# One decoder layer on one core: which engine makes the normalised x, and where in VectorE's queue it stands

## The chip, the cores and the metric

The kernel runs on one core of a Trainium2 chip. The metric is the device time of one execution in microseconds (us), as the median of several runs. The engines are TensorE (PE in the profile, its weight loads PEld), VectorE (DVE), ScalarE (ACT), GpSimd (POOL) and SyncE (SP, which issues the transfers). Each works through its own queue in order and waits on semaphores for the others.

## The reference

One layer of a decoder with 256 tokens and a model width of 1,024. The residual stream is normalised (RMSNorm) and multiplied by one wide matrix; the pieces of the product feed a mixture of dilated window attentions (A), a block attention (B), attention to 256 memory tokens (M), gates and merge logits. Cut to the part that the change touches:

```python
h = rmsnorm(x, norm_w[l])              # x * rsqrt(mean(x^2) + eps) * w
proj = h @ w_in[l]
pieces = jnp.split(proj, IN_SPLIT_POINTS, axis=-1)
...
kv = rmsnorm(mem, mem_norm_w[l]) @ w_mem_kv[l]
...
merged = g_a * p_a + g_b * p_b + g_m * p_m
x = x + merged @ w_out[l]
return rmsnorm(x, final_norm_w)
```

## The kernel before

Everything is fp32, but TensorE multiplies rounded values. So every operand `a` is split into a rounded upper part and the remainder, the lower part, and a product takes three matmuls: upper by upper, upper by lower, lower by upper. For a weight chunk, `split_cols` makes `wh` (upper, ScalarE, L93) and `wl` (lower, VectorE, L94).

The weights come in chunks of 1 MB, in the order of `PLAN` (L60). `load` (L79) issues a chunk's transfer three chunks ahead into one of three `wraw` buffers; `split` makes its upper and lower part in halves (from chunk 4 on) two chunks ahead. `wh` has three buffers and `wl` two, so `wl` of chunk i is written over that of chunk i-2. Chunks 0 to 5 are the query, key and value of branch B, two chunks each (`Bq`, `Bk`, `Bv`); 6 and 7 are gates of B, 8 to 10 gates of A and M, 11 and 12 the memory's key and value.

The normalisation needs a sum over the whole row, which is known late. Chunks 0 to 5 therefore multiply x times the norm's weights alone, `xh` and `xl` (L154, L155), and their results are scaled by the row's factor `rb["x"]` as they leave PSUM (`evac_b`, L546, L549, L541). From chunk 6 on the operand is the normalised x itself, `hh` and `hl`. `make_h` (L191) computes it into `h32`, one slice `k` of 128 features by 256 tokens at a time: x times the norm's weight of the feature `nw`, times the token's factor `rb`. Tokens are reordered on the way into four classes of position (`CLASSES`), so that both operands are read at every fourth element. Slices 0 and 1 are made on VectorE, in two halves each (L200); slices 2 to 7 on GpSimd in two steps, the weight in place (L196) and then the factor (L197). `split_h` (L203) splits four slices at a time: `hh` on ScalarE (L204), `hl` on VectorE (L205).

The loop over chunks (L554 on) calls, in iteration i: the transfer of chunk i+3; the first half of chunk i+2's split; the matmuls of chunk i, with the second half of the split between its two halves; and then, for the B chunks from 3 on, `evac_b`, at i = 3 `make_h` for all slices, and at i = 4 and 5 `split_h`. The order in which each engine's queue gets its instructions is not simply that of the program: it is settled when the program is built (L763), by a planner that goes by the program's order and by its own estimate of when each instruction can start. `x` transposed lies in `xp`, whose place is later taken by the memory `memT`; `h32` shares its place with the natural layouts of x before it and of the memory (`memn`) behind it. The two transfers of `mem_load` (L209) so wait for the last readers of x and `h32`.

Of the kernel before, what the change touches and what calls it, by code (L numbers as in the profile page):

```python
# [7 lines left out]
F32 = mybir.dt.float32  # L8
# [3 lines left out]
ALU = mybir.AluOpType  # L12
# [5 lines left out]
KD = D // P  # L18
# [9 lines left out]
CLASSES = "p (i r e) -> p e r i"  # L28
# [35 lines left out]
def kernel(ctx: ExitStack, tc: tile.TileContext, wts: bass.AP, xT_d: bass.AP, memT_d: bass.AP,  # L64
                      x_d: bass.AP, mem_d: bass.AP, xr_d: bass.AP, fnw_d: bass.AP, con_d: bass.AP, out: bass.AP):
    nc = tc.nc
# [5 lines left out]
    pa = ctx.enter_context(tc.tile_pool(name="pa", bufs=2, space=PSUM))  # L72

    NCH = len(PLAN)
    raws, whs, wls = {}, {}, {}
    width = [1024 if PLAN[i][0] == "W" and PLAN[i][2] == "m" else 2048 for i in range(NCH)]
    offs = [sum(width[:i]) * P for i in range(NCH + 1)]

# [8 lines left out]
    def split_cols(i, lo, hi):  # L87
        if lo == 0:
            o = place(i)
            whs[i] = wp.tile([P, 2112], F32R, tag="wh", name=f"wh{i}")[:, o:o + 2048]  # L90
            wls[i] = wp.tile([P, 2112], F32R, tag="wl", bufs=2, name=f"wl{i}")[:, o:o + 2048]
        sl = slice(lo, hi)
        nc.scalar.copy(whs[i][:, sl], raws[i][:, sl])  # L93
        nc.vector.tensor_tensor(wls[i][:, sl], raws[i][:, sl], whs[i][:, sl].bitcast(F32), op=ALU.subtract)  # L94

    def split(i, part, parts):
        n = width[i] // parts
        split_cols(i, part * n, (part + 1) * n)

    def place(i):  # L100


        return 32 if PLAN[i][0] in ("Av", "Bv", "Mv", "O") else 0
# [9 lines left out]
    par, xT = xp[:, 0:40], xp[:, 40:].rearrange("p (k t) -> p k t", k=KD)  # L113
    for i in range(2):
        raws[i] = wp.tile([P, 2048], F32, tag="wraw", name=f"wraw{i}")
        src0 = wts[offs[i]:offs[i + 1]].rearrange("(p c) -> p c", p=P)
        for j in range(4):
            k = 4 * i + j
# [21 lines left out]
    nw = par[:, 0:8]  # L140
# [12 lines left out]
    for k in range(KD):  # L153
        nc.scalar.activation(xh[:, k, :], xT[:, k, :], AF.Copy, scale=nw[:, k:k + 1])  # L154
        nc.vector.scalar_tensor_tensor(xl[:, k, :], xT[:, k, :], nw[:, k:k + 1], xh[:, k, :].bitcast(F32),  # L155
                                       op0=ALU.mult, op1=ALU.subtract)
        if k:
            split(k // 4, k % 4, 4)
        else:
            split(0, 0, 8)  # L160
            split(0, 1, 8)
# [29 lines left out]
    def make_h(lo, hi):  # L191
        rbp = rb["x"].rearrange(CLASSES, e=2, r=2)
        for k in range(lo, hi):
            hk = h32[:, k].rearrange("p e (r i) -> p e r i", r=2)
            if k >= 2:
                nc.gpsimd.tensor_scalar(xT[:, k, :], xT[:, k, :], nw[:, k:k + 1], 1.0, op0=ALU.mult, op1=ALU.mult)  # L196
                nc.gpsimd.tensor_tensor(hk, xT[:, k, :].rearrange(CLASSES, e=2, r=2), rbp, op=ALU.mult)  # L197
                continue
            for e in range(2):
                nc.vector.scalar_tensor_tensor(hk[:, e], xT[:, k, :].rearrange(CLASSES, e=2, r=2)[:, e], nw[:, k:k + 1],  # L200
                                               rbp[:, e], op0=ALU.mult, op1=ALU.mult)

    def split_h(lo, hi):  # L203
        nc.scalar.copy(hh[:, lo:hi], h32[:, lo:hi])  # L204
        nc.vector.tensor_tensor(hl[:, lo:hi], h32[:, lo:hi], hh[:, lo:hi].bitcast(F32), op=ALU.subtract)  # L205
# [67 lines left out]
    def split_q(src, scale, name):  # L273

        xs = []
        for s in range(2):
            own, other = halves(s)
            t = rp.tile([P, 512], F32R, tag="r", name=f"{name}x{s}")
            nc.scalar.mul(t[own], src[own], scale)
            nc.vector.scalar_tensor_tensor(t[other], src[own], scale, t[own].bitcast(F32), op0=ALU.mult,  # L280
                                           op1=ALU.subtract)
            xs.append(t)
        return [t.rearrange("p (f t) -> p f t", f=2) for t in xs]
# [269 lines left out]
    for i, (kind, key, src, col) in enumerate(PLAN):  # L553
# [54 lines left out]
        if kind[0] == "B":  # L608
            late.append((i, kind, key) + ((pss[2 * i], pss[2 * i + 1]) if i < 2 else (ps, None)))
            if i >= 3:  # L610
                for z in [z for z in late if i == 5 or z[0] > 1]:
                    evac_b(*z)
                    late.remove(z)
                if i == 3:
                    make_h(0, KD)
                else:
                    split_h(4 * i - 16, 4 * i - 12)
        elif kind in ("Aq", "Ak", "Av", "Mq", "Mk", "Mv"):
            at = (kind,) + (key if kind[0] == "A" else (0,))
            if kind[1] == "q" and at[-1] == 0:  # L620
                qkv[at] = split_q(ps, -SCALE, f"{kind}{i}")
            elif kind[1] == "k" and at[-1] == 0:
                qkv[at] = split_k(ps, f"{kind}{i}")
            elif kind == "Av" and key[1] > 0:

                hf, g = key
                if g == 1:
                    stacked[hf] = tp.tile([P, 2, 2, S], F32, tag="vs", name=f"vs{hf}")
                for r in range(2):
                    nc.scalar.copy(stacked[hf][64 * (g - 1):64 * g, :, r, :],  # L630
                                   ps[64 * r:64 * (r + 1)].rearrange("p (e c) -> p e c", e=2))
            else:
                t = qkv[at] = rtile(f"{kind}{i}")
                nc.scalar.mul(t, ps, -SCALE if kind == "Aq" else 1.0)
        elif kind == "G":
            th = tp.tile([P, 512], F32, tag="th", name="thg")
            nc.scalar.activation(th, ps, AF.Tanh, scale=0.5)
            g = gate[key] = rp.tile([P, 512], F32, tag="g", name=f"g{i}", bufs=5)
            nc.vector.scalar_tensor_tensor(g, th, 1.0, ps, op0=ALU.add, op1=ALU.mult)
        elif kind == "L":  # L640
            br, bk = key
            th = ths[br, bk] = tp.tile([P, 512], F32, tag="th", name="thl")
            off = {"a": 0, "b": 8, "m": 16}[br]
            for n in range(2):
                c = off + 2 * bk + n
                nc.scalar.activation(th[:, S * n:S * (n + 1)], ps[:, S * n:S * (n + 1)], AF.Tanh, bias=hb[:, c:c + 1],
                                     scale=0.5)
        elif kind == "W":
            br, hf = key
            kn = 2 if br == "m" else 4  # L650
            oh = [og[br, k][0] for k in range(kn)]
            ol = [og[br, k][1] for k in range(kn)]
            if "t" not in acc:
                acc["t"] = cp.tile([P, 4, 512], F32, tag="xt", name="acc")
            for j in range(2):
                bk = 2 * hf + j
                ps = pj.tile([P, 512], F32, tag="pj", name=f"pw{i}{j}")
                for n in range(2):
                    mm_feat(ps, S * n, i, kn, 512, 2 * j + n, oh, ol)
                    if j == 1 and n == 0 and i + 2 < NCH:  # L660
                        split(i + 2, 1, 2)
                a = acc["t"][:, bk, :]
                if br == "b":
                    nc.vector.scalar_tensor_tensor(a, ths[br, bk], 1.0, ps, op0=ALU.add, op1=ALU.mult)
                else:
                    tmp = tp.tile([P, 512], F32, tag="mt", name="mt", bufs=1)
                    nc.vector.scalar_tensor_tensor(tmp, ths[br, bk], 1.0, ps, op0=ALU.add, op1=ALU.mult)
                    if br == "m":
                        nc.gpsimd.tensor_tensor(a, a, tmp, op=ALU.add)
                    else:  # L670
                        nc.vector.tensor_tensor(a, a, tmp, op=ALU.add)
                        mh = rp.tile([P, 2, S], F32R, tag="r", name=f"mgh{bk}")
                        ml = rp.tile([P, 2, S], F32R, tag="r", name=f"mgl{bk}")
                        nc.scalar.copy(mh.rearrange("p a b -> p (a b)"), a)
                        nc.vector.tensor_tensor(ml.rearrange("p a b -> p (a b)"), a,
                                                mh.rearrange("p a b -> p (a b)").bitcast(F32), op=ALU.subtract)
                        merged[bk] = (mh, ml)
                if j == 0:
                    pump(i, 0)
        else:  # L680
            if key < 2:
                order = [(key, i, 0), (key, i, 1)]
            elif key == 2:
                order = [(key, i, 0)]
            else:
                order = [(key, i, 0), (key - 1, i - 1, 1), (key, i, 1)]
            with tc.manual_schedule(engines={mybir.EngineType.PE}) if key == 3 else ExitStack():
                for kc, wi, t in order:
                    out_mm(kc, wi, t)
                    if t == 0 and i + 2 < NCH:  # L690
                        split(i + 2, 1, 2)
                    if kc == 3:
                        finish(t)
# [73 lines left out]
```

## Time and profile before

| what | value |
| --- | --- |
| median of 3 runs | 355.07 us (354.67 to 355.75) |
| the profiled execution | 353.61 us |
| its span, first to last instruction | 351.8 us |
| mean granted TensorE clock | 0.991 |
| busy: TensorE, VectorE, ScalarE, GpSimd | 339.3, 237.0, 206.4, 35.1 us |

The profile is one execution. The span leaves out what lies before the first instruction and after the last. The granted clock is TensorE's, as a share of full speed. Matmuls overlap one another, so a matmul's duration is longer than the time from its start to the next one's.

### The profile page before, as it was taken

What the parts mean: (1) busy time and instruction counts of PE and PEld (TensorE: products, weight loads), DVE (VectorE), ACT (ScalarE), POOL (GpSimd) and SP (SyncE); (2) the same over time, 40 slices, a digit from 0 to 9 for tenths busy, and PEclk for the clock granted to TensorE, in tenths of its full rate; (3) what the DMA queues carried; (4) which work ended last, traced back from release to release, by engine and by line L of the source; (5) the groups of instructions that cost most, each with busy time, mean ns of one, the idle gap of its engine ahead of it and who ended that gap; (6) DMA issues with size and microseconds to landing.
All of it is one profiled execution on the core that took longest, in us unless ns stands there. A gap on an engine that the chain in (4) does not pass through costs nothing.

```text
span 351.8 us, 7109 instructions
## 1 busy us (share of the span) xinstructions
PE 339.3 (96%) x2924; PEld 324.5 (92%) x2924; DVE 237.0 (67%) x401; ACT 206.4 (59%) x367; POOL 35.1 (10%) x44
## 2 busy tenths in 40 slices
PE   8995999999999999999999999999999999999992
PEld 4995999999999998999999999999999999999882
DVE  3859979998898963446886352766544747567554
ACT  6665669867768664637766362864643465546222
POOL 1409200000001000000101000010000213000022
PEclk9999899999999999999999999999999999999998
DMA  7995695846334353445343635434334376645003
GB/s 211 312 411 197 259 386 202 322 149 232 129 126 153 135 203 118 168 136 224 122 132 115 228 126 197 164 129 159 133 121 169 132 241 238 234 143 224 0 2 120
DMA packets 12945, 63.33 MB, mean 180 GB/s; under 512 B 1392, under 2 KB 2800, under 8 KB 6640
## 3 DMA queue, kind: packets, MB, share of 16 engines
q1 hardware_dynamic: 12912, 62.88, 50.0%
q8 instruction: 23, 0.38, 0.4%
q14 instruction: 10, 0.08, 0.1%
HBM read 61.82 MB, written 1.05 MB: 179 GB/s over the span
## 4 chain that ended last, share of the span: by engine, by line
PE 88%; DMA 5%; DVE 3%; ACT 1%; SPq 1%; issue 0%; POOL 0%; POOLq 0%; DVEq 0%
PE pj L240 17%; PE pj L241 16%; PE pj L243 16%; PE pj L260 5%; PE pj L261 5%; PE pj L262 5%; PE pt L328 3%; PE pw L240 3%; DMA wraw<-in_wts 3%; PE pw L241 3%; PE pw L243 3%; DMA xn<-in_x 2%; PE y L501 2%; PE y L500 2%; PE y L499 2%; DVE h L200 1%
## 5 line engine op out<-in xcount | busy, mean ns | idle before, releaser
L94 DVE TENSOR_TENSOR wl<-wraw,wh 128x1024 fp32r<-128x1024 f32 (+2 forms) x117 | 131.5, 1159 | 65.1 <-issue 52.0
L93 ACT CAST wh<-wraw 128x1024 fp32r<-128x1024 f32 (+2 forms) x117 | 107.9, 967 | 45.9 <-PE pj L241 27.3
L240 PE MATMUL pj<-hh,wh 128*128 128x256 f32 x480 | 115.2, 281 | 0.0
L241 PE MATMUL pj<-hl,wh 128*128 128x256 f32 x480 | 113.8, 279 | 0.0
L240 PEld LDWEIGHTS pj<-hh,wh 128*128 128x128 f32 x480 | 90.4, 188 | 1.0 <-issue 0.6
L241 PEld LDWEIGHTS pj<-hl,wh 128*128 128x128 f32 x480 | 90.5, 188 | 0.4 <-issue 0.4
L243 PE MATMUL pj<-hh,wl 128*128 128x256 f32 x480 | 65.9, 279 | 0.0
L243 PEld LDWEIGHTS pj<-hh,wl 128*128 128x128 f32 x480 | 60.0, 188 | 0.0
L260 PE MATMUL pj<-wh,hh 128*128 128x256 f32 x96 | 27.0, 281 | 0.0
L262 PE MATMUL pj<-wh,hl 128*128 128x256 f32 x96 | 26.9, 280 | 0.0
L261 PE MATMUL pj<-wl,hh 128*128 128x256 f32 x96 | 26.7, 278 | 0.0
L320 ACT ACTIVATE u<-u,st 128x384 f32<-128x384 f32 (+2 forms) x32 | 16.9, 529 | 13.1 <-DVE st L314 13.1
L329 ACT COPY ptsb<-pt 128x384 f32<-128x384 f32 (+1 forms) x28 | 13.1, 495 | 11.4 <-PE pt L328 11.1
L260 PEld LDWEIGHTS pj<-wh,hh 128*128 128x128 f32 x96 | 18.1, 189 | 0.5 <-issue 0.4
L262 PEld LDWEIGHTS pj<-wh,hl 128*128 128x128 f32 x96 | 18.0, 188 | 0.4 <-issue 0.4
L261 PEld LDWEIGHTS pj<-wl,hh 128*128 128x128 f32 x96 | 18.0, 188 | 0.0
L362 POOL TENSOR_SCALAR nba<-con 128x512 f32<-128x512 f32 x8 | 5.0, 620 | 126.8 <-DVE st L314 125.9
L322 DVE TENSOR_SCALAR u<-u,st 128x256 f32<-128x256 f32 (+2 forms) x40 | 16.4, 416 | 0.9
L501 PE MATMUL y<-wh,mgl 128*128 128x512 f32 (+1 forms) x40 | 14.0, 350 | 0.0
L500 PE MATMUL y<-wl,mgh 128*128 128x512 f32 (+1 forms) x40 | 14.0, 350 | 0.0
L499 PE MATMUL y<-wh,mgh 128*128 128x512 f32 (+1 forms) x40 | 14.0, 349 | 0.0
L261 PE MATMUL pj<-wl,xh 128*128 128x256 f32 x32 | 9.9, 309 | 3.8 <-DVE wl L94 3.8
(196 smaller groups left out, 568.5 us busy)
## 6 DMA issues: line engine op xcount, KB each, us to landing
wraw<-in_wts SPq DMA_DIRECT2D x48, 1024.0 KB, 4.8
wraw<-in_wts SPq DMA_DIRECT2D x15, 256.0 KB, 6.1
xn<-in_x SPq DMA_DIRECT2D x1, 1024.0 KB, 8.4
memT<-in_memT SPq DMA_DIRECT2D x1, 1024.0 KB, 8.0
memn<-in_mem SPq DMA_DIRECT2D x1, 1024.0 KB, 8.6
xres<-in_xr SPq DMA_DIRECT2D x1, 1024.0 KB, 4.9
wraw<-in_wts SPq DMA_DIRECT2D x2, 512.0 KB, 3.2
out<-ysb SPq DMA_DIRECT2D x4, 256.0 KB, 2.1
```

The source lines that it names most:

```text
L93: nc.scalar.copy(whs[i][:, sl], raws[i][:, sl])
L94: nc.vector.tensor_tensor(wls[i][:, sl], raws[i][:, sl], whs[i][:, sl].bitcast(F32), op=ALU.subtract)
L240: nc.tensor.matmul(ps[:, lo:lo + S], wh[:, k, fs], ah[k], start=(k == 0), stop=False)
L241: nc.tensor.matmul(ps[:, lo:lo + S], wh[:, k, fs], al[k], start=False, stop=False)
L243: nc.tensor.matmul(ps[:, lo:lo + S], wl[:, k, fs], ah[k], start=False, stop=(k == kn - 1))
L260: nc.tensor.matmul(ps[:, lo:lo + S], ah[k], wh[:, k, :], start=(k == 0), stop=False)
L261: nc.tensor.matmul(ps[:, lo:lo + S], ah[k], wl[:, k, :], start=False, stop=False)
L262: nc.tensor.matmul(ps[:, lo:lo + S], al[k], wh[:, k, :], start=False, stop=(k == KD - 1))
L320: nc.scalar.activation(u[:, lo:hi], src[:, lo:hi], AF.Exp, bias=st[:, 0:1], scale=-1.0, accum_out=st[:, 1:2])
L499: nc.tensor.matmul(y[t, n][:, 0:w], ht, wh[:, k, cs], start=(kc == 0 and k == 0), stop=False)
L500: nc.tensor.matmul(y[t, n][:, 0:w], ht, wl[:, k, cs], start=False, stop=False)
L501: nc.tensor.matmul(y[t, n][:, 0:w], lt, wh[:, k, cs], start=False, stop=(kc == 3 and k == 1))
```

## The change

GpSimd multiplies all eight slices of x by the norm's weights, in place, in the loop that makes `xh` and `xl`. `make_h` has one VectorE instruction for a slice, whatever its number. It is called for four slices at i = 3 and for the other four at i = 4, and its VectorE instructions are put behind the last lower-part instruction of chunk i+1 in VectorE's queue (`issue_after`: an order within the queue, not a semaphore). At i = 4 `split_h` of the first four slices stands ahead of `make_h` of the last four.

```diff
-    raws, whs, wls = {}, {}, {}
+    raws, whs, wls, lower = {}, {}, {}, {}
...
-        nc.vector.tensor_tensor(wls[i][:, sl], raws[i][:, sl], whs[i][:, sl].bitcast(F32), op=ALU.subtract)
+        lower[i] = nc.vector.tensor_tensor(wls[i][:, sl], raws[i][:, sl], whs[i][:, sl].bitcast(F32), op=ALU.subtract)
...
         nc.vector.scalar_tensor_tensor(xl[:, k, :], xT[:, k, :], nw[:, k:k + 1], xh[:, k, :].bitcast(F32),
                                        op0=ALU.mult, op1=ALU.subtract)
+        nc.gpsimd.tensor_scalar(xT[:, k, :], xT[:, k, :], nw[:, k:k + 1], 1.0, op0=ALU.mult, op1=ALU.mult)
...
             hk = h32[:, k].rearrange("p e (r i) -> p e r i", r=2)
-            if k >= 2:
-                nc.gpsimd.tensor_scalar(xT[:, k, :], xT[:, k, :], nw[:, k:k + 1], 1.0, op0=ALU.mult, op1=ALU.mult)
-                nc.gpsimd.tensor_tensor(hk, xT[:, k, :].rearrange(CLASSES, e=2, r=2), rbp, op=ALU.mult)
-                continue
-            for e in range(2):
-                nc.vector.scalar_tensor_tensor(hk[:, e], xT[:, k, :].rearrange(CLASSES, e=2, r=2)[:, e], nw[:, k:k + 1],
-                                               rbp[:, e], op0=ALU.mult, op1=ALU.mult)
+            nc.vector.tensor_tensor(hk, xT[:, k, :].rearrange(CLASSES, e=2, r=2), rbp, op=ALU.mult)
...
-                if i == 3:
-                    make_h(0, KD)
-                else:
+                if i > 3:
                     split_h(4 * i - 16, 4 * i - 12)
+                if i < 5:
+
+                    with tc.issue_after(lower[i + 1].ins):
+                        make_h(4 * i - 12, 4 * i - 8)
```

## Rows read from the trace of the kernel before

**Rows 1.** The page: busy time of each engine, its share of the span, instructions.

```profile
PE 339.3 (96%) x2924; PEld 324.5 (92%) x2924; DVE 237.0 (67%) x401; ACT 206.4 (59%) x367; POOL 35.1 (10%) x44
```

**Rows 2.** TensorE's waits: engine, line, whom it waited for; total us, times, longest.

```profile
PE pj L261 <- DVE wl L94: 3.8, 1, 3.8
```

**Rows 3.** Stretches of the span: length, busy time of each engine, clock, transfers.

```profile
core 0: us, PE busy (x) PEld busy (x) DVE busy (x) ACT busy (x) POOL busy (x), PEclk, DMA share, GB/s
...
22.90:30.40 7.50, 6.91 (x55) 6.45 (x54) 6.64 (x11) 4.93 (x9) 4.41 (x4) 1.00 1.00 389
30.40:34.20 3.80, 0.05 (x1) 0.05 (x1) 3.80 (x4) 2.11 (x3) 3.80 (x4) 1.00 0.17 69
34.20:38.40 4.20, 4.20 (x22) 4.16 (x23) 4.20 (x4) 3.77 (x4) 3.61 (x3) 0.59 0.21 59
...
47.00:66.00 19.00, 19.00 (x168) 18.95 (x167) 18.47 (x25) 18.50 (x28) 0.71 (x1) 1.00 0.75 271
```

**Rows 4.** Timeline of TensorE: start, duration (us), instruction, [idle before it, its releaser].

```profile
23.95 0.38 PE L240 MATMUL pj<-xh,wh 128*128 128x256 f32 x1 [0.58 <-ACT wh L93]
...
30.11 0.28 PE L260 MATMUL pj<-wh,xh 128*128 128x256 f32 x1
34.15 0.39 PE L261 MATMUL pj<-wl,xh 128*128 128x256 f32 x1 [3.76 <-DVE wl L94]
...
46.21 0.28 PE L262 MATMUL pj<-wh,xl 128*128 128x256 f32 x1
...
47.04 0.28 PE L240 MATMUL pj<-hh,wh 128*128 128x256 f32 x1
...
77.28 0.28 PE L241 MATMUL pj<-ml,wh 128*128 128x256 f32 x1
```

**Rows 5.** Timeline of ScalarE.

```profile
26.59 2.00 ACT L93 CAST wh<-wraw 128x1024 fp32r<-128x1024 f32 x2
...
57.60 1.06 ACT L171 ACTIVATE memn<-memn 128x1024 f32<-128x1024 f32 x1
```

**Rows 6.** Timeline of VectorE, instructions of one kind in a row merged.

```profile
27.33 4.67 DVE L200 SCALAR_TENSOR_TENSOR h<-xp,rb_x 128x128 f32<-128x128 f32 x4
...
37.47 0.68 DVE L549 SCALAR_TENSOR_TENSOR Bk<-pj,rb_x 128x512 f32<-128x512 f32 x1
38.06 2.35 DVE L94 TENSOR_TENSOR wl<-wraw,wh 128x1024 fp32r<-128x1024 f32 x2
40.33 1.21 DVE L205 TENSOR_TENSOR hl<-h,hh 128x1024 fp32r<-128x1024 f32 x1
...
42.66 1.41 DVE L546 SCALAR_TENSOR_TENSOR Bq<-pj,rb_x 128x256 f32<-128x256 f32 x4
...
47.17 2.36 DVE L94 TENSOR_TENSOR wl<-wraw,wh 128x1024 fp32r<-128x1024 f32 x2 [1.97 <-issue]
...
67.56 3.25 DVE L224 SCALAR_TENSOR_TENSOR memT<-memT,small,rb_m 128x256 f32<-128x256 f32 x8
...
74.80 1.30 DVE L228 TENSOR_TENSOR ml<-memT,mh 128x512 fp32r<-128x512 f32 x2
```

**Rows 7.** Single instructions of VectorE and GpSimd in the timeline, 30 to 36 us.

```profile
30.67 1.33 DVE L200 SCALAR_TENSOR_TENSOR h<-xp,rb_x 128x128 f32<-128x128 f32 x1
30.47 1.29 POOL L197 TENSOR_TENSOR h<-xp,rb_x 128x256 f32<-128x256 f32 x1
...
31.92 2.17 DVE L94 TENSOR_TENSOR wl<-wraw,wh 128x1024 fp32r<-128x1024 f32 x1
31.73 1.29 POOL L197 TENSOR_TENSOR h<-xp,rb_x 128x256 f32<-128x256 f32 x1
...
34.02 2.19 DVE L94 TENSOR_TENSOR wl<-wraw,wh 128x1024 fp32r<-128x1024 f32 x1
```

**Rows 8.** Instructions of L196: shortest, median, longest in ns, first and last start.

```profile
L196 POOL TENSOR_SCALAR xp<-xp x6: 477/667/880, 8.3 to 15.2; 128x256 f32<-128x256 f32 x6
```

**Rows 9.** Timeline of the queue that issues transfers.

```profile
41.58 0.38 SPq L211 DMA_DIRECT2D memn<-in_mem  x1
```

**Rows 10.** The page's transfers: size, median us from issue to landing.

```profile
memn<-in_mem SPq DMA_DIRECT2D x1, 1024.0 KB, 8.6
```

## The prediction

> **What bounds the kernel now.** I read the page first, then the waits of TensorE, then the stretches around the one long wait, then the queues one by one.
>
> TensorE is busy for 339.3 us, 96% of the span [rows 1], so time can be won only where TensorE waits or runs slowly. The list of its waits names one long wait in the whole span: 3.8 us, for the lower part `wl` of a weight chunk, on VectorE [rows 2]. The table by stretch shows it at 30.4 to 34.2 us: TensorE does one instruction, VectorE and GpSimd are busy throughout. [...]
>
> TensorE's own timeline says what it waited for. At 30.11 us it starts chunk 4 (`Bv`, first half) with the product of upper parts (L260); the next product (L261) needs `wl` of chunk 4 and comes at 34.15 us. Chunk 6, the first to need `hh` and `hl`, starts at 47.04 us [rows 4].
>
> VectorE's queue says why `wl` was late. ScalarE rounds chunk 4's upper part from 26.59 to 28.6 us [rows 5], so `wl` could start at about 27.6. VectorE's program order, however, has four L200 instructions first: 4.67 us from 27.33 [rows 6], while GpSimd makes the other six slices. `wl` of chunk 4 starts at 31.92, and its two halves take 2.17 and 2.19 us [rows 7], where two halves of a later chunk take 2.35 us together [rows 6].
>
> The single records of the two engines show them taking turns. GpSimd's L197 instructions start at 30.47 and 31.73, VectorE's at 30.67 and 31.92 [rows 7]. Both records of 1.3 us are mostly waiting: between 30.47, when one GpSimd instruction ended, and 30.67, when VectorE's ended, VectorE had 0.20 us; again 0.19 us between 31.73 and 31.92. GpSimd had 30.67 to 31.73, which is 1.06 us. So a strided half slice (128 columns) is worth about 0.2 us on VectorE alone, and a strided slice (256 columns) about 1.06 us on GpSimd.
>
> **The change part by part.**
>
> *GpSimd's multiplication by the norm's weights.* Six such instructions exist already; they run between 8.3 and 15.2 us, 0.48 to 0.88 us each [rows 8]. The edit adds two, for slices 0 and 1, at the same place. They work in place, behind the two readers of the slice. At worst each holds up one VectorE instruction by its own 0.48 us; no wait of TensorE for `wl` is listed but the one of chunk 4 [rows 2], so there is room for that. Cost: 0. Without that cover it would be up to 2 × 0.48 = 1.0 us.
>
> *GpSimd's six L197 products go.* This takes away VectorE's partner in the turns: `wl` of chunk 4 falls from 2.17 + 2.19 = 4.36 to 2.35 us.
>
> *VectorE's eight products.* The trace has no unshared strided product of 256 columns. Lower bound: contiguous columns, eight instructions of the same size with two SBUF tensors in 3.25 us, 0.41 each [rows 6]; the turns above would give two halves for 2 × 0.2 = 0.4. Upper bound: L200's record at face value, 1.33 us for a single instruction [rows 7]; taken per half that would be 2.66, which only repeats GpSimd's share of the time. I take 0.41, 1.63 us for each half of x, as both nearest readings agree.
>
> [...]
>
> *The order on VectorE.* The first four products are now queued behind the second half of chunk 4's `wl`, the last four behind that of chunk 5's. The first half of `wl` can start at 27.6 us and both are done by 27.6 + 2.35 = 30.0 us. TensorE wants them from 30.23 on. The wait of 3.76 us [rows 4] goes.
>
> *What the slow stretch gives back.* With no idle stretch the clock has no reason in this trace to fall: in the 7.5 us before, with a wait of 0.58 us inside, it stayed 1.00 [rows 3, 4]. In 34.2 to 38.4 us a granted 0.59 means 4.2 × 0.41 = 1.7 us lost.
>
> Sum: 3.76 + 1.72 = 5.5 us. Check: seven matmuls of this stage take 47.04 − 46.21 = 0.83 us [rows 4], 0.119 each; the 96 matmuls of chunks 4 and 5 from 30.11 then end at 41.5 instead of 47.04, 5.5 us earlier.
>
> *What is late next.* TensorE reaches chunk 6 at 41.5 us, and there needs `hh` and `hl`. VectorE's list from 27.6 us: `wl` of chunks 4, 5, 6 (three times 40.33 − 38.06 = 2.27), products 3.25, one `Bk` 0.59 (38.06 − 37.47), `hl` twice 1.21, `Bq` 1.41 [rows 6]: 6.81 + 3.25 + 0.59 + 2.42 + 1.41 = 14.5, done at 42.1 us. The second half of `hl` is wanted nine matmuls after 41.5, at about 42.5. It fits, with little room. ScalarE is no obstacle: from 28.6 us it has two chunks of `wh` at 2.0 us and two `hh`, each as wide as half a chunk, 1.0 us [rows 5]: 6 us of work in 13.
>
> Behind it, `wl` of chunk 7 starts at 47.17 us [rows 6], 0.13 us after TensorE leaves chunk 5, whose buffer it takes, so it moves with TensorE. From there to 66 us VectorE is busy for 18.47 and ScalarE for 18.50 of 19.0 us [rows 3]: lateness there is not made good. A delay of 0.6 us (42.1 against 41.5) would be carried to the memory's `ml`, finished at 76.10 us and wanted at 77.28 [rows 4, 6]: 1.2 us of room, enough.
>
> *The queue of transfers.* `memT` waits for the last reader of x, `memn` for the last reader of `h32`; the weights behind them in the queue wait too. `memn` is issued at 41.58 us [rows 9]. By the list above `h32` is read to the end by 42 us, much as now, so it stays about where it is, while TensorE is 5.5 us nearer. `memn`'s first user, the squares on ScalarE, starts at 57.60 us, 16.0 us behind the issue [rows 5, 9]; it would come 10.5 us behind it, still after the 8.6 us that `memn` takes to land [rows 10]. Cost: 0; it would cost what the transfer is late, if it took over 10.5 us.
>
> Behind 42 us no wait of TensorE is in the list [rows 2], so what is won at 41.5 is kept to the end.
>
> **The sum and the median.** The profiled execution took 353.61 us; less 5.5 it is 348.1. The median of the runs shown is 355.07, 1.46 us above the profiled one; against it the forecast is 349.6 us.
>
> **The rivals.**
>
> *Forecast:* the wait and the slow stretch go, little comes back. 349.6 us, with 0.8 us to either side. Chance 0.70.
>
> *Part comes back as a new wait on VectorE.* The room is 0.4 us at chunk 6 and 0.6 at `ml`. The order of the queues is settled anew when the program is built; if `hl` stands behind `wl` of chunk 7, or the products wait for ScalarE's rounding while `wl` is behind them, TensorE waits 1 to 4 us at chunk 5, 6 or 11. For it: VectorE is full from 47 to 66 us. Against: the list fits with every piece counted. 350.5 to 353.5 us. Chance 0.17.
>
> *The strided products are dear, and the time goes up.* At 0.41 + d each, eight cost 8d more; at most 0.6 us is hidden, the rest stalls TensorE at chunk 6, and a stall like the present one brings 1.7 us of slow clock again. It breaks even where 8d − 0.6 + 1.7 = 5.5, at d = 0.55, 0.96 us a product. At GpSimd's 1.06 it is 0.8 us slower than before; at 1.33, taking L200's record at its word, 8 × 0.92 − 0.6 + 1.7 − 5.5 = 3.0 us slower, 358.1. For it: the records, read plainly. Against: two turns of 0.2 us for half a slice. Chance 0.06.
>
> [...]
>
> *The change does not do what it says.* Chunk 4's `wl` may stay late, if `wh` or something else not ordered by the edit is now ahead of it in a queue; a wait of the same size stands elsewhere, 355.1 us. Against: `wh` was ready 3 us early. Chance 0.07.
>
> **How the numbers follow.** A difference of 0.3%, 1.07 us, is about what a measurement of this kernel can tell from none. Faster: the forecast and the second case, 0.87. No change: most of the last, 0.06. Slower: the third and a remainder, 0.07. The range takes in the forecast's own (348.8 to 350.4), a little below it for the spread of the runs, and two thirds of the second case: 348.5 to 352.5.
>
> **What would show it.** Right: no TensorE wait at chunk 4; a granted clock of 1.00 from 22.9 to 47 us; `wl` of chunk 4 started near 27.6 with pieces of about 1.2 us; eight products of 0.4 us each; chunk 6 started near 41.5. Wrong: products of 0.9 us or more; a TensorE wait for `hl`, `wl` or `ml` of over 1 us before 72 us; a clock under 1.00 behind it.

## The result, and the profile after

The median of six runs is 350.47 us (349.53 to 351.44), beside 354.32 us (353.77 to 355.75) for six runs of the kernel before: a ratio of 0.9881, 95% interval 0.9862 to 0.9900. The kernel is faster, by 1.2%. The profiled execution took 350.43 us, with a span of 348.6 and a mean granted clock of 0.997.

Line numbers have moved a little: `make_h` is L196, `split_h` L199 and L200, matmuls by features L235, L236, L238, by tokens L255 to L257, `memT` L219, `ml` L223, the copy `rb_m` L184, `Bk`'s evacuation L544. First the page's busy row and TensorE's waits, which answer to [rows 1, 2].

```profile
PE 339.3 (97%) x2924; PEld 324.2 (93%) x2924; DVE 233.0 (67%) x405; ACT 207.0 (59%) x367; POOL 27.1 (8%) x40
```

```profile
engine line waited for: us in total, times, longest us
...
PE pj L235 <- ACT wh L93: 0.7, 1, 0.7
PE pj L256 <- DVE wl L94: 0.4, 1, 0.4
PE pj L248 <- ACT wh L93: 0.4, 1, 0.4
PE pj L236 <- DVE ml L223: 0.3, 1, 0.3
PE pj L235 <- DVE ssq_m L144: 0.2, 1, 0.2
```

The wait of 3.8 us is gone; three small ones for VectorE have come. The stretches of [rows 3] again, with the same columns:

```profile
22.90:30.40 7.50, 6.83 (x57) 6.57 (x56) 6.36 (x11) 5.29 (x10) 2.46 (x3) 1.00 1.00 386
30.40:34.20 3.80, 3.80 (x34) 3.80 (x34) 3.80 (x7) 3.27 (x4) 0.00 (x0) 1.00 0.86 306
34.20:38.40 4.20, 4.20 (x38) 4.20 (x37) 4.20 (x7) 3.00 (x5) 0.00 (x0) 1.00 0.54 191
...
47.00:66.00 19.00, 18.82 (x163) 18.70 (x162) 18.80 (x40) 16.02 (x30) 1.63 (x3) 1.00 0.82 310
```

TensorE is busy throughout 30.4 to 38.4 us, at a granted clock of 1.00. In its timeline `wl` of chunk 4 follows `wh` at once, and chunk 6 starts at 41.41 us, where it started at 47.04 [rows 4]: 5.63 us earlier.

```profile
30.10 0.28 PE L255 MATMUL pj<-wh,xh 128*128 128x256 f32 x1
30.22 0.28 PE L256 MATMUL pj<-wl,xh 128*128 128x256 f32 x1
...
41.41 0.28 PE L235 MATMUL pj<-hh,wh 128*128 128x256 f32 x1
```

At the end of the span 3.2 us are left of the 5.6. VectorE's timeline shows the first reason.

```profile
27.70 2.69 DVE L94 TENSOR_TENSOR wl<-wraw,wh 128x1024 fp32r<-128x1024 f32 x2 [0.28 <-ACT wh L93]
30.31 2.23 DVE L196 TENSOR_TENSOR h<-xp,rb_x 128x256 f32<-128x256 f32 x4
32.46 0.68 DVE L544 SCALAR_TENSOR_TENSOR Bk<-pj,rb_x 128x512 f32<-128x512 f32 x1
33.06 2.35 DVE L94 TENSOR_TENSOR wl<-wraw,wh 128x1024 fp32r<-128x1024 f32 x2
35.33 2.22 DVE L196 TENSOR_TENSOR h<-xp,rb_x 128x256 f32<-128x256 f32 x4
...
43.30 2.38 DVE L94 TENSOR_TENSOR wl<-wraw,wh 128x1024 fp32r<-128x1024 f32 x2
```

Four products take 32.46 − 30.31 = 2.15 us, 0.54 each. `wl` of chunk 4 takes 30.31 − 27.70 = 2.61 us, where that of chunk 5 takes 35.33 − 33.06 = 2.27 (GpSimd's L414, 27.58 to 29.3 us, runs beside the first; that this is the reason was not tested). `wl` of chunk 7 starts at 43.30, 1.9 us after TensorE left chunk 5; it was 0.13 [rows 4, 6].

TensorE's own order changed too, though no line of the edit names it: the planner put the first scores of the block attention (`sb`) before chunk 9, where they stood in the middle of chunk 11. The first row is from before, the second from after:

```profile
75.28 0.28 PE L304 MATMUL sb<-Bk0y,Bq0x 128*128 128x256 f32 x1
58.41 0.28 PE L299 MATMUL sb<-Bk0y,Bq0x 128*128 128x256 f32 x1
```

The second reason lies around 60 to 77 us. The fence holds, of the timeline, the queue that issues transfers, then ScalarE, VectorE and TensorE.

```profile
56.60 0.38 SPq L557 DMA_DIRECT2D xres<-in_xr  x1
58.92 9.46 SPq L85 DMA_DIRECT2D wraw<-in_wts  x3
...
65.99 2.00 ACT L93 CAST wh<-wraw 128x1024 fp32r<-128x1024 f32 x2 [1.32 <-DMA wraw<-in_wts]
...
68.38 0.36 ACT L184 COPY rb_m<-spread_m 128x256 f32<-128x256 f32 x1
...
58.81 0.68 DVE L636 SCALAR_TENSOR_TENSOR g<-thg,pj 128x512 f32<-128x512 f32 x1
...
69.12 3.25 DVE L219 SCALAR_TENSOR_TENSOR memT<-memT,small,rb_m 128x256 f32<-128x256 f32 x8
...
59.18 0.27 PE L300 MATMUL sb<-Bk0z,Bq0x 128*128 128x128 f32 x1
59.63 0.36 PE L235 MATMUL pj<-hh,wh 128*128 128x256 f32 x1 [0.18 <-DVE ssq_m L144]
...
73.50 0.28 PE L235 MATMUL pj<-mh,wh 128*128 128x256 f32 x1
74.17 0.39 PE L256 MATMUL pj<-wl,mh 128*128 128x256 f32 x1 [0.39 <-DVE wl L94]
...
76.39 0.27 PE L300 MATMUL sb<-Bk1z,Bq1x 128*128 128x128 f32 x1
76.96 0.39 PE L236 MATMUL pj<-ml,wh 128*128 128x256 f32 x1 [0.29 <-DVE ml L223]
```

Chunk 12's transfer, issued at 58.92 behind `xres` (1 MB that is wanted only at the end), lands at about 66. ScalarE waits 1.32 us for it, with the copy `rb_m` queued behind its rounding, and `memT`, `ml` and chunks 11 and 12 behind the copy. At 59 us it is VectorE alone: there are three `pj` buffers in PSUM, so chunk 9 takes that of chunk 6, which VectorE reads for the gate `g` until 59.49, behind its late list (the profile puts this wait down to `ssq_m`, VectorE's next instruction). A stall is here what a step from one matmul to the next has over a yardstick, where that is over 0.2 us. The yardstick is an estimate from TensorE's timeline of before: at a granted clock of 0.50, from 36.64 to 37.92 us, six steps of 256 columns take 1.28 us, 0.213 each, which at 1.00 would be 0.107; for 128 columns half of that is taken. (Of the steps of 256 columns in the profiles of before and after, 92% take 0.113 to 0.120 us.) The stalls are 0.40 at 59.18, 0.26 at 72.72, 0.56 at 73.50, 0.52 at 76.39. Together 1.74 us.

For the experiments one measure is used beside the times: from chunk 6's first product to the last matmul's end. What goes before, the start with its wait for chunk 3's `wh`, varies by 2 us and more from one profiled execution to the next (in the seven profiles of kernels that begin as the changed one, chunk 4 starts between 29.8 and 31.7 us, in one at 33.6). In the kernel before this measure is 345.65 − 47.04 = 298.61 us, after it 342.47 − 41.41 = 301.06: 2.45 us given back.

### The profile page after: what moved, and what is told of

Read it like the earlier page. It is cut to its first block, busy times and chain, and to the rows that moved or that the text cites. A ratio compares the mean times of both kernels' runs of the same rounds, so it can differ in the third digit from the quotient of the medians.

```text
span 348.6 us, 7107 instructions
## 1 busy us (share of the span) xinstructions
PE 339.3 (97%) x2924; PEld 324.2 (93%) x2924; DVE 233.0 (67%) x405; ACT 207.0 (59%) x367; POOL 27.1 (8%) x40
## 3 DMA queue, kind: packets, MB, share of 16 engines
HBM read 61.82 MB, written 1.05 MB: 180 GB/s over the span
## 4 chain that ended last, share of the span: by engine, by line
PE 86%; DMA 6%; DVE 2%; SPq 2%; issue 1%; ACT 1%; POOL 0%; POOLq 0%; DVEq 0%; ACTq 0%
PE pj L235 16%; PE pj L236 16%; PE pj L238 16%; PE pj L255 5%; PE pj L257 5%; PE pj L256 5%; DMA wraw<-in_wts 4%; PE pw L235 3%; PE pt L323 3%; PE pw L238 3%; PE pw L236 3%; DMA xn<-in_x 2%; PE y L496 2%; PE y L495 2%; PE y L494 2%
## 5 line engine op out<-in xcount | busy, mean ns | idle before, releaser
L94 DVE TENSOR_TENSOR wl<-wraw,wh 128x1024 fp32r<-128x1024 f32 (+2 forms) x117 | 129.8, 1146 | 66.2 <-issue 50.1
L235 PE MATMUL pj<-hh,wh 128*128 128x256 f32 x480 | 115.2, 281 | 0.2 <-DVE ssq_m L144 0.2
L236 PE MATMUL pj<-hl,wh 128*128 128x256 f32 x480 | 114.5, 279 | 0.0
L235 PEld LDWEIGHTS pj<-hh,wh 128*128 128x128 f32 x480 | 90.3, 188 | 1.3 <-issue 0.6
L236 PEld LDWEIGHTS pj<-hl,wh 128*128 128x128 f32 x480 | 90.4, 188 | 0.4 <-issue 0.4
L238 PE MATMUL pj<-hh,wl 128*128 128x256 f32 x480 | 66.6, 279 | 0.0
L238 PEld LDWEIGHTS pj<-hh,wl 128*128 128x128 f32 x480 | 60.3, 188 | 0.0
L255 PE MATMUL pj<-wh,hh 128*128 128x256 f32 x96 | 27.0, 281 | 0.0
L257 PE MATMUL pj<-wh,hl 128*128 128x256 f32 x96 | 26.8, 280 | 0.0
L255 PEld LDWEIGHTS pj<-wh,hh 128*128 128x128 f32 x96 | 18.1, 189 | 0.5 <-issue 0.4
L257 PEld LDWEIGHTS pj<-wh,hl 128*128 128x128 f32 x96 | 18.0, 188 | 0.4 <-issue 0.4
L317 DVE TENSOR_SCALAR u<-u,st 128x256 f32<-128x256 f32 (+2 forms) x40 | 15.1, 398 | 0.6
L323 PE MATMUL pt<-con,u 128*128 128x128 f32 x88 | 13.0, 274 | 0.0
```

The source lines that it names most:

```text
L94: lower[i] = nc.vector.tensor_tensor(wls[i][:, sl], raws[i][:, sl], whs[i][:, sl].bitcast(F32), op=ALU.subtract)
L235: nc.tensor.matmul(ps[:, lo:lo + S], wh[:, k, fs], ah[k], start=(k == 0), stop=False)
L236: nc.tensor.matmul(ps[:, lo:lo + S], wh[:, k, fs], al[k], start=False, stop=False)
L238: nc.tensor.matmul(ps[:, lo:lo + S], wl[:, k, fs], ah[k], start=False, stop=(k == kn - 1))
L255: nc.tensor.matmul(ps[:, lo:lo + S], ah[k], wh[:, k, :], start=(k == 0), stop=False)
L257: nc.tensor.matmul(ps[:, lo:lo + S], al[k], wh[:, k, :], start=False, stop=(k == KD - 1))
```

## The experiments

Two explanations of the 2.4 us stood against each other. One: VectorE's list was longer than worked out, and VectorE, full to 66 us, carries its lateness to chunks 9 to 12. The other: the memory's chain (squares, `rb_m`, `memT`, `ml`) is held up by the order of the queues and by a transfer, whatever VectorE did before 47 us. The letters in the expectations stand for theories as each of them states them. Ratios are against the kernel before on the same chip, with 95% intervals.

**e1_order_only: the order without the change of engine.** The kernel before, with its products behind chunk 4's `wl`:

```diff
...
-                    make_h(0, KD)
+                    with tc.issue_after(lower[4].ins):
+                        make_h(0, KD)
```

> The order alone: engines as in the kernel before (GpSimd makes six slices, VectorE two in halves), but VectorE's four instructions are queued behind chunk 4's wl. Theory (both parts are needed): the wait at chunk 4 goes, since wl's halves then take turns with GpSimd and end near 29 and 31.2 us; but VectorE's four pieces, each waiting its turn behind a GpSimd product of 1.06 us, end only near 36 us, wl of chunk 5 near 38 to 39, and TensorE waits some 2 us at chunk 5: 351 to 353 us. Rival (the order is the whole change): no wait at chunk 5, as fast as the changed kernel, 350.5 or less.

352.69 us, 0.9929 (0.9900 to 0.9958). Chunk 4's wait is gone, and comes back one chunk later, with the clock behind it (waits, then stretches):

```profile
PE pj L261 <- DVE wl L94: 2.0, 1, 2.0
```

```profile
35.70:38.00 2.30, 0.30 (x4) 0.09 (x2) 2.30 (x4) 1.70 (x2) 1.16 (x3) 1.00 0.27 61
38.00:42.20 4.20, 4.20 (x24) 4.20 (x25) 4.20 (x6) 4.20 (x7) 0.00 (x0) 0.65 0.94 369
```

**e2_engine_only: the engine without the order.** The changed kernel, but all eight products at i = 3, queued freely:

```diff
+                if i == 3:
+                    make_h(0, KD)
+                else:
                     split_h(4 * i - 16, 4 * i - 12)
-                if i < 5:
-                    with tc.issue_after(lower[i + 1].ins):
-                        make_h(4 * i - 12, 4 * i - 8)
```

> The engine alone: VectorE makes all eight slices, but all at once and not queued behind wl, so that they stand ahead of chunk 4's wl as L200 did. Theory: eight products at the 0.54 us that the changed kernel's trace shows take 4.3 us from 27.3, wl of chunk 4 starts near 31.7 and its first half ends near 32.8 instead of 34.1 us; TensorE still waits about 2.5 us and the slow clock may follow: 352 to 354 us. Rival (the removal of GpSimd's products is what pays): 350.5 or less.

353.78 us, 0.9952 (0.9924 to 0.9980). In the profile, which is of the slowest of its executions (355.87 us), TensorE waits at chunk 4, and the granted clock is 0.64 from 35.6 to 39.8 us:

```profile
PE pj L256 <- DVE wl L94: 1.8, 1, 1.8
```

So each half of the change alone leaves a wait of about 2 us with a low clock behind it; only both together take it away.

**e3_rb_first: ScalarE's copy first.** The changed kernel, with ScalarE's rounding of chunk 12 behind its copy `rb_m`; this alone is different in any queue.

```diff
...
+            with tc.issue_after(rbm[0].ins) if i == 10 else ExitStack():
+                for j in range(2 if i < 2 else 1):
+                    split(i + 2, j, 4 if i < 2 else 2)
...
+                        with tc.issue_after(rbm[0].ins) if i == 10 else ExitStack():
+                            split(i + 2, 1, 2)
```

> The changed kernel with one move: on ScalarE the two wh pieces of chunk 12 stand behind the copy of the memory's row factor rb_m instead of ahead of it; nothing else in any queue differs. Theory A (the gain is given back at chunks 11 and 12 because VectorE is late there, with the first attention pair's softmax pulled ahead): VectorE's memT products start only some 0.6 us sooner (about 68.5), since wl of chunk 11 is ahead of them, and 0.3 to 0.7 us of the span comes back. Theory B (it is given back because rb_m stands behind a transfer that is late): the waits at 72 to 77 us go, 1.5 us or more comes back, span near 347.0.

350.48 us, 0.9871 (0.9844 to 0.9897). Chunk 6 to the end: 300.43 us, 0.63 under the profile of the changed kernel. That looks like theory A, but it is only 0.11 under e5 below, the changed kernel profiled once more, and the median is the changed kernel's: a gain of this move is not shown. Theory B's 1.5 us did not come.

**e4_softmax_later: the first pair's softmax behind the memory.** VectorE's softmax of the first pair of heads behind the last `ml`:

```diff
...
+                with tc.issue_after(memst["last"].ins) if pair == 0 else ExitStack():
                     softmax(banks[s], nb[:, 0:S], us[s], 0, S)
                     softmax(banks[s], nb[:, P:S], us[s], S, S + P)
```

> The changed kernel with VectorE's part of the first attention pair's softmax queued behind the last of the memory's ml. Theory A: VectorE loses 3.3 us of work ahead of ml, the TensorE waits between 58 and 78 us go, and the span falls by 1.5 to 2.2 us to about 346.5, 348.5 us in time. Theory B: rb_m is still behind chunk 12's wh, the waits stay, span 348 to 349.

353.04 us, 0.9938 (0.9913 to 0.9962): worse by 2.6 us than the changed kernel; this remedy missed. ScalarE's timeline says why the room on VectorE was of no use: the copy still stood behind the rounding of chunk 12, and that behind its transfer.

```profile
66.40 2.00 ACT L93 CAST wh<-wraw 128x1024 fp32r<-128x1024 f32 x2 [4.26 <-DMA wraw<-in_wts]
68.30 0.37 ACT L184 COPY rb_m<-spread_m 128x256 f32<-128x256 f32 x1
```

TensorE stalled at chunks 9, 11 and 12, 2.8 us in four places, and chunk 6 to the end took 302.96 us. The planner also reordered other work, so this run shows only that moving the softmax away did not bring the memory earlier.

**e5_after_again, e6_contiguous, e7_permuted, e8_permuted_rb_first.** The changed kernel again; the same with both operands read in natural order (e6, whose h comes out in the wrong order of tokens); and a kernel that computes the whole reference (e7): GpSimd writes x times the weights in class order into a buffer of its own, and a copy of `rb_x` in class order, so that VectorE reads columns one after another. e8 adds the edit of e3. The core of e7 (the transfer of `memT`, which no longer waits for the products, is kept at its place in the queue):

```diff
-        nc.gpsimd.tensor_scalar(xT[:, k, :], xT[:, k, :], nw[:, k:k + 1], 1.0, op0=ALU.mult, op1=ALU.mult)
+        nc.gpsimd.tensor_scalar(xw[-1][:, k % 2], xT[:, k, :].rearrange(CLASSES, e=2, r=2), nw[:, k:k + 1], 1.0, op0=ALU.mult, op1=ALU.mult)
...
+                        nc.gpsimd.tensor_scalar(rb["c"], rb["x"].rearrange(CLASSES, e=2, r=2), 1.0, 1.0, op0=ALU.mult, op1=ALU.mult)
...
-            nc.vector.tensor_tensor(hk, xT[:, k, :].rearrange(CLASSES, e=2, r=2), rbp, op=ALU.mult)
+            nc.vector.tensor_tensor(hk, xw[k // 2][:, k % 2], rb["c"], op=ALU.mult)
```

> The changed kernel once more, as the yardstick for the three kernels that run beside it. Both theories: 0.988 of the kernel before, chunk 6 started near 41.4 us, eight products at 0.54 us from start to start, VectorE's lower part of chunk 7 started near 43.3 us, a lead over the kernel before of 5.6 us at chunk 6 and of 3.2 us from 105 us on.

> The changed kernel with both operands of the eight products read in natural order, column after column; it leaves out the reordering into classes, so its h is in the wrong order, and every instruction and every queue is as in the changed kernel. Theory A (the stride made the products dear, 0.54 instead of 0.41 us, and the late VectorE carries that to the memory's chunks): products of 0.40 to 0.41 us, the lower part of chunk 7 on VectorE 1.0 us earlier, and of the 2.4 us given back between 47 and 105 us some 0.5 to 1.0 us less: 0.5 to 1.0 us under the changed kernel. Theory B (0.54 is the price of two SBUF operands in this stretch, stride or none): products of 0.5 us or more and the same time. Theory C (the memory chain loses the time by its own order, whatever VectorE did before 47 us): products of 0.40, chunk 7 earlier, and the same time within 0.3 us.

> The changed kernel with GpSimd writing x times the norm's weights into a buffer of its own, already in class order, and making a copy of rb_x in class order, so that VectorE's eight products read columns one after another; the order of all queues is the same but for that one copy on GpSimd. It computes the whole reference. Theory A: as the contiguous kernel, products of 0.40 to 0.41 us and 0.5 to 1.0 us under the changed kernel, if GpSimd's strided multiplies (0.5 to 1.1 us each, between 8 and 17 us) and its copy of rb_x stay hidden. Theory C: the time of the changed kernel. Rival: GpSimd's strided work holds up the lower parts of chunks 0 to 2 on VectorE and TensorE waits there, 0.3 to 1 us over the changed kernel.

> The permuted kernel, and ScalarE's rounding of chunk 12 queued behind its copy of rb_m. It computes the whole reference. Theory A: VectorE is 1.0 us less late and the copy of rb_m, no longer behind the rounding that waits for its transfer, gives back 0.3 to 0.7 us more: 1.0 to 1.7 us under the changed kernel, a lead over the kernel before of 4.2 to 4.9 us from 105 us on. Theory C: 0.3 to 0.7 us under the changed kernel.

Times: 350.47, 350.49, 350.39 and 349.72 us; ratios 0.9871 (0.9849 to 0.9893), 0.9874 (0.9847 to 0.9901), 0.9871 (0.9849 to 0.9892), 0.9856 (0.9831 to 0.9881). By the medians, taking away the stride gives nothing that these runs can tell, as theory C had it; theory A's 0.5 to 1.0 us (1.0 to 1.7 for e8) did not come. The traces say more. VectorE's timeline of e6:

```profile
31.89 1.42 DVE L196 TENSOR_TENSOR h<-xp,rb_x 128x256 f32<-128x256 f32 x4
33.24 0.67 DVE L544 SCALAR_TENSOR_TENSOR Bk<-pj,rb_x 128x512 f32<-128x512 f32 x1
...
47.78 0.68 DVE L292 TENSOR_TENSOR Bk0z<-Bk,Bk0y 64x512 fp32r<-64x512 f32 x1 [0.70 <-ACT Bk0y L286]
```

Without the stride a product is worth (33.24 − 31.89) / 4 = 0.34 us, less than any theory had. The stride costs 0.20 us each, 1.6 us for eight. Of these 1.6 us VectorE at once loses 0.70 to ScalarE, which is next to be late; e7 and e8 show the same wait (0.69). What is left is enough for the stall at 59 us: it is 0.40, 0.36 and 0.39 us in the changed kernel, e5 and e3, and below 0.1 in e6, e7 and e8. VectorE is done with chunk 6's gate 18.0 to 18.1 us after the start of chunk 6 in the first three, and 17.15 us after it in the others. The stalls at chunks 11 and 12 do not follow the stride: 1.34 us in the changed kernel, 0.31 in e5 (the same program), 2.02 in e6 (the profile is of its slowest execution), 0.21 in e7, none in e8. They follow the transfer of chunk 12, which lands 7.0, 6.5, 8.2 and 6.8 us after its issue in the first four. There ScalarE starts its rounding within 0.1 us of the landing, and `memT` starts 3.13 us after the rounding, each time: 65.99 and 69.12, 65.12 and 68.25, 67.83 and 70.96, 65.87 and 69.00 us. In e8, where the copy does not stand behind the rounding, the transfer took 6.7 us and cost nothing; in e3 it took only 5.0 us, so that there was hardly a delay to take away.

**e9_xres_later, e10_permuted_xres_later, e11_permuted_all.** The transfer of `xres` behind chunk 24's weights, in the changed kernel (e9), in e7 (e10) and in e8 (e11):

```diff
+            with tc.issue_after(loads[24].ins):
                 nc.sync.dma_start(xres, xr_d.rearrange("(t p) d -> p t d", p=P))
```

> The changed kernel with one transfer moved in the queue of transfers: xres, 1 MB that is wanted only at the end, goes behind chunk 24's weights and no longer between chunks 11 and 12; all compute queues are as in the changed kernel. Theory D (with TensorE 5.6 us nearer, chunk 12's weights are late: xres stands ahead of them, ScalarE's rounding of chunk 12 waits for them, its copy of rb_m stands behind that rounding, and memT, ml and chunk 11 behind the copy): chunk 12's transfer lands 4 to 5 us after its issue instead of 7, ScalarE waits for it no longer, rb_m is copied 0.7 to 1.2 us earlier against chunk 4, and 0.3 to 0.7 us are gained on the changed kernel: ratio 0.986. Theory A (VectorE's late list alone): the copy is earlier, memT stays behind the lower part of chunk 12 on VectorE, and the time stays that of the changed kernel, 0.987 to 0.988.

> The permuted kernel with the same transfer moved. It computes the whole reference. If VectorE's late list and chunk 12's late transfer are two causes of one delay, each hidden by the other, both together gain about 1.3 us on the changed kernel, 0.984 to 0.9855, with no wait of TensorE over 0.2 us between 47 and 84 us; if the transfer was no cause, the permuted kernel's own 0.987.

> The permuted kernel with xres moved and with ScalarE's rounding of chunk 12 behind its copy of rb_m. It computes the whole reference. With xres moved chunk 12's weights are there in time, so the order of rounding and copy is worth at most 0.5 us: 0.983 to 0.986, and no wait of TensorE over 0.2 us between 47 and 84 us.

350.25, 350.38 and 349.52 us; 0.9855 (0.9830 to 0.9879), 0.9880 (0.9842 to 0.9917), 0.9838 (0.9814 to 0.9861). Theory D's 0.986 and theory A's 0.987 to 0.988 both lie in e9's interval, so the traces have to decide. ScalarE in e9 no longer waits for the transfer, and `rb_m` comes at 66.82 us instead of 68.38 (1.34 us earlier against the start of chunk 4; 0.81 earlier than in e5). With no `xres` ahead, chunk 12 lands 4.9, 4.9 and 5.2 us after its issue in e9, e10 and e11; with it, in the six profiles above, it took 5.0 to 8.2. ScalarE's timeline of e9:

```profile
64.43 2.00 ACT L93 CAST wh<-wraw 128x1024 fp32r<-128x1024 f32 x2
66.33 0.59 ACT L635 ACTIVATE thg<-pj 128x512 f32<-128x512 f32 x1
66.82 0.36 ACT L184 COPY rb_m<-spread_m 128x256 f32<-128x256 f32 x1
```

The stalls at chunks 11 and 12 are gone in e9, though VectorE's list is as late as in the changed kernel (`wl` of chunk 7 starts 1.92 us after chunk 6, there 1.90). The one at 59 us, which is VectorE's alone, is 0.93 us. In e10 and e11 both are gone (0.1 us at most). Two of e10's six runs took 353.1 and 353.5 us; they were not profiled, so its ratio settles nothing. All waits of TensorE in e11:

```profile
PE pj L251 <- ACT wh L93: 1.1, 3, 0.5
PE pwarm L138 <- DVE zero L109: 1.0, 1, 1.0
```

e11 computes the whole reference and is the best kernel of the study, 349.52 us (349.09 to 350.33); 0.95 us under the changed kernel's 350.47 by the medians, though the two were not measured side by side.

The table puts the profiles side by side, in us: from chunk 6 to the end; the stall at chunk 9; from the start of `spread_m` on TensorE to that of `memT` on VectorE; the stalls at chunks 11 and 12.

```
kernel                  chunk 6 to end   chunk 9   spread_m to memT   chunks 11, 12
before                      298.61         0            3.50               0
after                       301.06         0.40         3.15               1.34
e5_after_again              300.54         0.36         2.48               0.31
e3_rb_first                 300.43         0.39         2.52               0.34
e6_contiguous               301.31         0            3.81               2.02
e7_permuted                 299.90         0            2.40               0.21
e8_permuted_rb_first        299.78         0            2.28               0
e9_xres_later               300.46         0.93         2.30               0
e10_permuted_xres_later     299.79         0            2.27               0
e11_permuted_all            299.78         0            2.28               0
```

Two columns explain most of what sets the changed versions apart in the first; each row is one execution. The stall at chunk 9 is there with the strided products and gone without them. The stalls at 11 and 12 grow with the time that the memory's chain takes, from none at 2.3 us to 2.02 at 3.81 (the kernel before could afford 3.50, for it started chunk 11 10.65 us after `spread_m`; the changed kernel starts it 6.4 us after it). Less its stalls, each changed version needs 299.3 to 299.9 us.

## Why the prediction was right, and where it was off

**The wait and the clock: right.** The wait of 3.76 us and the low clock behind it (0.59 over the 4.2 us of [rows 3]; within them 0.50 from 34.86 to 38.27 us, and 1.00 from 30.00 to 34.85 and from 38.28 to 75.00) went, worked out as 5.5 us; chunk 6 started 5.63 us earlier, at 41.41 for the 41.5 forecast. `wl` of chunk 4 started at 27.70 (27.6), and the granted clock stayed 1.00. e1 and e2 show that order and engine are both needed.

**The forecast's time.** Against the profiled execution it was 353.61 − 5.5 = 348.1, and 350.43 was measured: 2.3 us off. The 349.6 on record comes nearer to the 350.47 only by luck, because the median that it was made against, 355.07, lay higher than the 354.32 of the six runs; from there the gain is 3.85 us, not 5.5. What happened is nearest to the second case, part of the gain coming back as waits before 77 us, at its lower edge of 350.5. Its mechanism is only half of what came: the waits stood at chunks 9, 11 and 12, and those at 11 and 12 did not come from VectorE's late list.

**The term that was mis-sized: VectorE's list.** "I take 0.41" was 0.54 us a product, 4.26 instead of 3.25 us for eight; `wl` of chunk 4 added 0.3. The list ended at 43.3 instead of 42.1 us, and a delay of 1.9 instead of 0.6 us was carried on. What it cost is the stall at chunk 9, 0.40 us here and 0.93 in e9; at the memory's `ml`, where the prediction looked for it, e9 shows no stall with the same delay. The nearest rows were misleading on both sides: half slices in turn with GpSimd looked like 0.4 us for a slice, and the contiguous instruction of 0.41 was of another form; the same form without the stride takes 0.34. The stride has its price here, 0.54 beside 0.34 us. It did not turn the sign, as break-even was worked out at 0.96.

**Room that was read from TensorE's old order.** The prediction has the second half of `hl` wanted at about 42.5 us and `ml` 1.2 us before its use. `hl` was done only at 43.41, and still TensorE hardly waited (one step of 0.16 us, at 43.53). That was luck: its order in chunk 6 had changed as well. Two `hh` products stand in a row at 42.35, where `hh` and `hl` took turns before, and the first product with `wl` comes 2.99 us after chunk 6's start (44.40) instead of 1.83 (48.87 before).

```profile
42.17 1.24 DVE L200 TENSOR_TENSOR hl<-h,hh 128x1024 fp32r<-128x1024 f32 x1
42.35 0.40 PE L235 MATMUL pj<-hh,wh 128*128 128x256 f32 x2
```

At `ml` the new order took room away: chunk 11 starts 6.4 us after `spread_m` instead of 10.65. What the old order with the change would have cost was not tried.

**The step that failed: "Cost: 0" for the transfers, and "what is won at 41.5 is kept to the end".** The prediction followed `memn` and `memT`, and both were in time. The transfer that became late was another one, chunk 12's weights behind `xres`: 7.0 us from issue to landing, where it takes about 4.9 with no `xres` ahead. With TensorE 5.6 us nearer, ScalarE waited 1.32 us for it with `rb_m` behind, and 1.34 us of stalls followed at chunks 11 and 12. Neither cause could be told from the waits alone, which name `wl`, `ml` and `ssq_m` on VectorE. e9 took the delay of the transfer away and left VectorE's stall, e7 the other way round nearly so, e11 both. This rests on the traces, one for each kernel; the medians (350.25, 350.39 and 349.52 beside 350.47) are too near to each other to show the parts.

**The sum.** 5.63 won; stalls of 0.40 + 1.34 = 1.74 back; and 0.65 us in which nothing waits (below). 5.63 − 1.74 − 0.65 = 3.24, and the spans are 351.8 − 348.6 = 3.2 apart.

**GpSimd's two extra multiplies: nothing seen.** No wait of TensorE for `wl` ahead of chunk 4 is in the list of the changed kernel, and chunk 4 starts at 30.10 us, as before at 30.11.

## What to carry to other kernels

When a stall goes, list for each engine what comes in the tens of microseconds behind it, the transfers that nobody waited for included: a load behind a less urgent one in the same queue can be late as soon as its consumer is early (here chunk 12 behind `xres`, 7.0 us from issue to landing instead of about 4.9). Where a planner settles the order, read room from the order of the new kernel: two of the rooms here were read from the old one, and one held only because the order had changed. A strided operand is worth a measurement in the same form of instruction (here 0.54 us with the stride and 0.34 without), and work that has slack (here GpSimd's multiply) can write the permuted order for the engine that has none. Where the medians can't tell versions apart, compare the traces from a fixed instruction on, and keep a run-to-run wait at the start out of the comparison.

## What the runs showed of the hardware that was not expected

TensorE's matmuls of 256 columns follow one another in one of two rhythms, 0.113 or 0.118 us, both at a granted clock of 1.00, and keep to one for dozens of matmuls (147 steps in a row of the shorter one in the kernel before, 128 of the longer one in the changed kernel). The same eight products of chunk 6 in the timelines of before and of after:

```profile
48.87 1.07 PE L243 MATMUL pj<-hh,wl 128*128 128x256 f32 x8
49.77 0.28 PE L240 MATMUL pj<-hh,wh 128*128 128x256 f32 x1
```

```profile
44.40 1.10 PE L238 MATMUL pj<-hh,wl 128*128 128x256 f32 x8
45.34 0.28 PE L235 MATMUL pj<-hh,wh 128*128 128x256 f32 x1
```

(49.77 − 48.87) / 8 = 0.1125 us, (45.34 − 44.40) / 8 = 0.1175. The kernel before keeps the shorter step from 47.3 us nearly to 75 us; the changed kernel has the longer one until the stall at 59.18 us and for three steps behind it, and the shorter one from 60.18 to 65.74. e1 shows the cost without any wait: TensorE's order is that of the kernel before, and so is the granted clock, yet from chunk 6 to the last matmul it takes 299.66 us instead of 298.61. The stretches from chunk 6 to 80 us, of before and of e1:

```profile
47.04:80.00 32.96, 32.96 (x290) 32.91 (x289) 32.38 (x53) 27.83 (x45) 1.11 (x2) 1.00 0.68 249
```

```profile
45.07:80.00 34.93, 34.93 (x297) 34.88 (x296) 34.01 (x60) 29.08 (x49) 1.52 (x3) 1.00 0.66 244
```

In both TensorE is busy throughout. The 150th matmul behind chunk 6's first comes 17.01 us after it in the kernel before and 17.67 in e1, the 250th 28.60 and 29.65 us; from there on the difference stays 1.05 us to the end. That is about 0.0043 us a matmul. Some 150 matmuls of 256 columns lie between 41.41 and 59.18 us in the changed kernel; at 0.0043 us each, an estimate, they cost it 0.65 us. What sets the rhythm was not found and not tried; by the same estimate it is 0.7 of the 1.2 us that e11 still needs over the kernel before from chunk 6 on (299.78 and 298.61); the other 0.5 us stay open.
